# Token rows ahead of the rank matmuls, RWKV keys and solves by halves of the heads, nine loads ahead of a branch

## The chip, the cores and the metric

The kernel runs on one core of one Trainium2 chip. The metric is device time in microseconds from launch to end, the median of several runs. A profiled execution, taken beside them, shows what each engine did: TensorE (PE, with its weight loads PEld), VectorE (DVE), ScalarE (ACT), GpSimd (POOL) and SyncE (SP, which issues most DMA transfers).

## The reference

A block of two layers over 256 latent tokens and 256 context tokens of width 1024, all in float32. Layer 0 mixes the tokens by attention, layer 1 by RWKV-7, and each is followed by a mixture of 16 experts of which a token uses two. Cut to what the change touches:

```python
# after each mixer, on all tokens (512 in layer 0, the 256 latent ones in layer 1)
hl = modulate(rmsnorm(xl, norm_ffn_g[i]), ml[3], ml[4])
probs = softmax(h @ router_w)                       # 16 experts
sel   = (probs + router_bias)                       # choose a group, then two experts in it
expert_idx, gate_w = route(tokens, router_w, router_bias)
f = moe_ffn(tokens, expert_idx, gate_w, w1, w3, w2) # (silu(x @ w1) * (x @ w3)) @ w2 per expert

# RWKV: 16 heads of 64, two directions, state S of 64 x 64 per head
r, k, v = mix(0) @ w_r, mix(2) @ w_k, mix(3) @ w_v
kk = k * k_k, normalised per head
for each direction d, token t:
    sa = S @ (-kk_t)
    S  = S * decay_t + outer(sa, kk_t * iclr_t) + outer(v_t, k_d_t)
    y_t = S @ r_t
```

The kernel does not run that recurrence token by token. It cuts the 512 tokens of each direction into chunks of 64; within a chunk the products of the decayed `kk` with `kk * iclr` form a triangular 64 x 64 matrix per head, which is inverted, and a scan over the chunks uses the inverses.

## The kernel before, in words

The program is written as a sequence of stages, and a scheduler that simulates the engines orders each engine's queue from it; the order in which the stages are written decides most of it, and rotating buffers the rest.

*Routing and token rows (`route`, `moe`).* `route` (line 606) takes the router's logits, transposes them (L611), and on VectorE runs a chain of some forty small operations to the chosen experts as one-hot rows `ob` (L662). The rank matmuls (L669), 14 in layer 0 and 5 in layer 1, count how many tokens ahead of each chose the same expert. `moe` then makes the *token rows*: for each tile `t` of 128 tokens (four in layer 0, two in layer 1) and each half `n` of the width, a diagonal matrix `dg` of the norm's factors times the rows (L854, in layer 1 L857), in layer 0 plus a one-row product that adds the shift (L855), copied by ScalarE to `mhh`, and its rounding remainder by a subtraction on PE (L859) to `mhl`. The gather (L1877, L1878 in layer 0; L1049, L1050 in layer 1) picks the rows of each expert with one-hot matmuls, and so needs all token rows.

*Experts of layer 0 (`experts0`).* 16 experts in an order that the data decides, the first eight with room for 128 tokens, the others 64. Weights come in loads of 1 MB (L132, on SP's queue) into a ring of nine buffers, are split into a high and a low part (ScalarE L139, VectorE L140) for the first eight, and go to PE (L145 to L147, L1896). After the twelfth of them (`a == 11`) stands `overflow` (line 932): a conditional block (L939) for tokens over an expert's room, which is not entered with this data, but every engine evaluates its flag, and SP's queue is drained there.

*RWKV.* The string list at line 1177 is the order of the stages: `l` the low-rank projections, `K`, `R`, `V` projections, `H0` to `H3` the decayed tensors ("hats") and their products for the four tiles `u` of 128 tokens (`wkv_hat`), `S0` to `S3` the triangular solves, one for a tile with all 16 heads (`wkv_solve`), `c0` to `c7` the scan over chunks, `M` and `n` the output. The products (L1566) use 64 of the 128 columns of PE; the two chunk halves `lc` of a tile go one after the other to the same columns and into a PSUM tile each. A solve copies the products to VectorE's layout with a transpose (L1593), does 31 steps of a multiplication (L1600) and an addition (L1602), transposes twice (L1604, L1605), and ends with two rounds of small matmuls (L1624, L1628). The hats' products L1653 of the scan alternate between the two halves of the columns.

*Order around the changes.* SP issues loads in program order and stops at the first one whose buffer is not free. All engines run their queues in order.

Of the kernel before, what the change touches and what calls it, by code (L numbers as in the profile page):

```python
# [79 lines left out]
class Net:  # L80
# [525 lines left out]
    def route(self, wk, layer, T):  # L606
# [18 lines left out]
        V.tensor_tensor(out=lg, in0=p2[:, :32 * T].rearrange("p (t e) -> p t e", t=T)[:, :, 0:16], in1=bc(rs), op=ALU.mult)  # L625
        lv = lg.rearrange("p (v t) e -> p v t e", t=2)
# [200 lines left out]
    def moe(self, layer, sf):  # L827
        nc, I, F = self.nc, self.I, self.ffn
        T, cap, t0 = (4, 128, 0) if layer == 0 else (2, 64, 2)
        with ExitStack() as sm:  # L830
# [4 lines left out]
            with ExitStack() as s:  # L835
# [6 lines left out]
                r = self.route(F["rp"], layer, T)  # L842
# [4 lines left out]
                for t in range(T):  # L847
                    dg = wk.tile([128, 128], F32, tag="dg", bufs=2, name=self.uid("dg"))
                    nc.scalar.activation(dg, self.ident, AF.Copy, scale=rs[:, t:t + 1])
                    for n in range(2):  # L850
# [8 lines left out]
                        nc.tensor.matmul(p, neg, hh[:, t, ns], start=False, stop=True, skip_group_check=True)  # L859
                        nc.scalar.activation(hl[:, t, ns], p, AF.Copy)  # L860
            sf.close()
# [267 lines left out]
    def rwkv(self, st, se, sf):  # L1129
# [41 lines left out]
        self.AB, V, y = [], [], []  # L1171
# [5 lines left out]
        for o in ["l", "K", "h", "H0", "R", "H1", "Vm", "gate", "V", "hx", "close", "S0", "S1", "c0", "H2", "c1", "H3", "x", "S2", "S3", "c2", "c3", "M4", "n", "c4", "M5", "c5", "M6", "c6", "M7", "c7", "F"]:  # L1177
# [23 lines left out]
            elif o == "K":  # L1201
                self.proj_k(h)
# [10 lines left out]
            elif o[0] == "H":  # L1213
                q = int("0011"[u])
                self.AB.append(vp[q].tile([128, 2, 16, 64], F32, tag="AB", bufs=2 if q == 0 else 2, name=self.uid("AB")))
                self.wkv_hat(u, self.AB[-1])
            elif o[0] == "S":
                self.wkv_solve(vp[int("0101"[u])], u, self.AB[u])
# [111 lines left out]
    def proj_k(self, h):  # L1330
        mh, ml = self.mix_split(2, h)
        for n in range(4):
# [163 lines left out]
    def wkv_hat(self, u, AB):  # L1496
# [3 lines left out]
        for d in range(2):  # L1500
# [9 lines left out]
            for kh in range(2):  # L1510
                wk = self.hp[(2 * d + kh) % len(self.hp)]
                ks = slice(4 * kh, 4 * kh + 4)
                kk = self.ht(wk, "kk", [128, 2, 4, 128])
                nc.sync.dma_start(out=kk, in_=self.kks[:, :, ks, seg, ts])
                if lat:
                    rr = self.ht(wk, "rr", [128, 4, 128])
# [494 lines left out]
```

## Time and profile before

| | us |
|---|---|
| median of three runs | 2009.86 (2005.5 to 2012.11) |
| profiled execution | 2008.92 |
| its span, first to last instruction | 2007.1 |
| mean granted clock of TensorE | 0.93 |

The stages in the profile's time, from the span's start: conditioning and attention 0 to 325; first routing and token rows 325 to 372; experts of layer 0 372 to 935; RWKV 935 to 1505 with its projections to 1198 and solves and scan to 1452; second routing, rows and branch 1505 to 1532; experts of layer 1 to the end.

A row of a stretch gives the busy time of each engine in it. The granted clock is the share of full speed that TensorE was given: 1.00 is 2.4 GHz, 0.50 is 1.2 GHz, what lies between is a mean over both. The DMA share is the mean busy share of the 16 DMA engines. In a row in time, the text in brackets is the idle time of the engine just before, and who ended it.

### The profile page before, as it was taken

What the parts mean: (1) busy time and instruction counts of PE and PEld (TensorE: products, weight loads), DVE (VectorE), ACT (ScalarE), POOL (GpSimd) and SP (SyncE); (2) the same over time, 40 slices, a digit from 0 to 9 for tenths busy, and PEclk for the clock granted to TensorE, in tenths of its full rate; (3) what the DMA queues carried; (4) which work ended last, traced back from release to release, by engine and by line L of the source; (5) the groups of instructions that cost most, each with busy time, mean ns of one, the idle gap of its engine ahead of it and who ended that gap; (6) DMA issues with size and microseconds to landing.
All of it is one profiled execution on the core that took longest, in us unless ns stands there. A gap on an engine that the chain in (4) does not pass through costs nothing. (4 is left out here: it accounts for less than half of the span.)

```text
span 2007.1 us, 30401 instructions
## 1 busy us (share of the span) xinstructions
PE 1741.1 (87%) x11729; PEld 1060.6 (53%) x11729; DVE 957.7 (48%) x1801; ACT 738.0 (37%) x1432; POOL 318.9 (16%) x306
## 2 busy tenths in 40 slices
PE   5979998999999998995699897889967999988986
PEld 3845574665556556552277777778753333322321
DVE  2466654465555555456843688985453111110101
ACT  2234542454454544442554777643132010000000
POOL 1040031000000000005455635330230000000000
PEclk7989997799999998998698998889978999999999
DMA  8376863289999996994455779754295999999996
GB/s 328 105 295 254 268 177 112 93 337 409 406 410 355 395 410 252 385 410 185 115 189 188 249 220 273 215 142 97 86 396 201 409 409 409 409 409 409 409 409 268
DMA packets 229570, 577.04 MB, mean 287 GB/s; under 512 B 42859, under 2 KB 87171, under 8 KB 229413
## 3 DMA queue, kind: packets, MB, share of 16 engines
q1 hardware_dynamic: 212726, 543.48, 73.4%
q10 hardware_dynamic: 15536, 27.28, 3.8%
q0 software_dynamic: 1152, 4.19, 0.6%
q8 instruction: 97, 1.59, 0.3%
q14 instruction: 59, 0.48, 0.1%
HBM read 537.38 MB, written 37.54 MB: 286 GB/s over the span
## 5 line engine op out<-in xcount | busy, mean ns | idle before, releaser
L140 DVE TENSOR_TENSOR lo<-raw,hi 128x512 fp32r<-128x512 f32 x456 | 301.2, 710 | 207.5 <-ACT hi L139 201.5
L139 ACT ACTIVATE hi<-raw 128x512 fp32r<-128x512 f32 x488 | 289.2, 627 | 167.2 <-PE ps L147 116.4
L1063 PE MATMUL ps<-raw,XT 128*64 128x512 f32 x1024 | 234.3, 597 | 16.7 <-DMA raw<-in_moe_w_dram 16.7
L1063 PEld LDWEIGHTS ps<-raw,XT 128*64 128x64 f32 x1024 | 72.0, 136 | 172.5 <-issue 123.1
L1069 DVE TENSOR_TENSOR h<-h,ps 128x512 f32<-128x512 f32 x16 | 11.0, 687 | 306.2 <-PE ps L1063 306.2
L1081 PE MATMUL ps<-raw,hT 128*64 128x512 f32 x512 | 118.7, 600 | 16.0 <-DVE hT L1074 9.4
L1896 PE MATMUL ps<-raw,XT 128*64 128x512 f32 x512 | 120.7, 602 | 0.2 <-DMA raw<-in_moe_w_dram 0.2
L145 PE MATMUL ps<-hi,xh 128*128 128x512 f32 x256 | 101.1, 415 | 18.8 <-ACT hi L139 11.5
L146 PE MATMUL ps<-lo,xh 128*128 128x512 f32 x256 | 105.6, 412 | 1.7 <-DVE lo L140 1.6
L147 PE MATMUL ps<-hi,xl 128*128 128x512 f32 x256 | 102.7, 401 | 0.0
L886 POOL DMA_INDIRECT yk<-ybuf,cidx x8 | 7.8, 972 | 596.0 <-issue 596.0
L256 POOL TENSOR_TENSOR rs<-rs,mh 128x2 f32<-128x2 f32 (+2 forms) x5 | 4.3, 851 | 528.2 <-DVE rs L255 528.1
L1081 PEld LDWEIGHTS ps<-raw,hT 128*64 128x64 f32 x512 | 34.7, 136 | 79.6 <-issue 52.8
L145 PEld LDWEIGHTS ps<-hi,xh 128*128 128x128 f32 x256 | 49.3, 195 | 44.2 <-ACT hi L139 20.6
L224 PE MATMUL ps<-raw,cv 128*32 128x256 f32 x768 | 62.2, 425 | 9.4 <-DMA raw<-in_ada_w_dram 5.9
L1896 PEld LDWEIGHTS ps<-raw,XT 128*64 128x64 f32 x512 | 32.4, 136 | 60.1 <-issue 57.1
L146 PEld LDWEIGHTS ps<-lo,xh 128*128 128x128 f32 x256 | 49.8, 194 | 25.6 <-DVE lo L140 8.2
L1068 ACT ACTIVATE h<-ps 128x512 f32<-128x512 f32 x16 | 9.6, 597 | 143.1 <-PE ps L1063 143.1
L1085 ACT ACTIVATE ye<-ps 128x512 f32<-128x512 f32 x16 | 9.6, 597 | 140.1 <-PE ps L1081 140.1
L1896 PE MATMUL ps<-raw,hT 128*64 128x512 f32 x256 | 58.7, 599 | 0.8 <-DVE hT L1952 0.8
L145 PE MATMUL ps<-hi,th 128*128 128x512 f32 x128 | 48.4, 406 | 8.6 <-ACT hi L139 8.5
L147 PEld LDWEIGHTS ps<-hi,xl 128*128 128x128 f32 x256 | 49.9, 195 | 9.6
(471 smaller groups left out, 3570.4 us busy)
## 6 DMA issues: line engine op xcount, KB each, us to landing
raw<-in_moe_w_dram SPq DMA_DIRECT2D x384, 1024.0 KB
raw<-in_ada_w_dram SPq DMA_DIRECT2D x48, 1024.0 KB
kk<-kks SPq DMA_DIRECT2D x16, 512.0 KB
hB<-BK SPq DMA_DIRECT2D x16, 512.0 KB
BKm<-hB SPq DMA_DIRECT2D x16, 512.0 KB
raw<-in_attn_w_in_dram SPq DMA_DIRECT2D x6, 1024.0 KB
raw<-in_attn_w_out_dram SPq DMA_DIRECT2D x8, 512.0 KB
ybuf<-ye ACTq DMA_DIRECT2D x8, 512.0 KB
```

The lines of the kernel that those rows point to most:

```text
L139: nc.scalar.activation(hi, src, AF.Copy)
L140: (lo_eng or nc.vector).tensor_tensor(out=lo, in0=src, in1=hi.bitcast(F32), op=ALU.subtract)
L145: mm(out, lh, rh, start=start, stop=False, skip_group_check=True)
L146: mm(out, lh, rl, start=False, stop=False, skip_group_check=True)
L147: mm(out, ll, rh, start=False, stop=stop, skip_group_check=True)
L224: nc.tensor.matmul(p[32 * q:32 * q + 32, :], self.cv[:, k, :], w[:, a, q * 256:(q + 1) * 256], start=(k == 0), stop=(k == KT - 1), skip_gr ...
L1063: nc.tensor.matmul(acc[64 * n:64 * n + 64, :], XT[:, k, e % 4 * 64:e % 4 * 64 + 64], w[:, a, n * 512:(n + 1) * 512], start=(k == 0), stop= ...
L1068: nc.scalar.activation(h, hs[0], AF.Silu)
L1069: nc.vector.tensor_tensor(out=h, in0=h, in1=hs[1], op=ALU.mult)
L1081: nc.tensor.matmul(acc[64 * n:64 * n + 64, :], hT[:, k % 4, (k // 4) * 64:(k // 4) * 64 + 64], w[:, a, n * 512:(n + 1) * 512], start=(k == ...
L1085: nc.scalar.activation(ye, acc, AF.Copy)
L1896: nc.tensor.matmul(acc[0][64 * n:64 * n + 64, :], lhs(k), w[:, a, ns], start=(k == 0), stop=(k == KT - 1), skip_group_check=True)
```

## The change

Three edits. First, `route` takes a function `rows(t)` that makes the token rows of tile `t`; it issues the first half of the tiles ahead of the rank matmuls, and the second half behind them, held in that order by `issue_after`. Second, in RWKV the projection of the keys, the hats and the solves are cut by halves of the heads (`kh`): a solve now covers eight heads of two tiles (`S00`, `S01` for tiles 0 and 1, `S10`, `S11` for 2 and 3) instead of sixteen of one, so that each has the same size; the products of both chunk halves `lc` go into one PSUM tile, to partitions 0 to 63 and 64 to 127, in alternation. Third, nine loads are issued ahead of the overflow branch.

```diff
     def route(self, wk, layer, T, rows):
 ...
+        last = [rows(t) for t in range(T // 2)][-1]
         lv = lg.rearrange("p (v t) e -> p v t e", t=2)
 ...
-        for t in range(T + 1):
-            for u in range(min(t + 1, T)):
-                nc.tensor.matmul(pk[:, t, :], bf[:, 0 if u == t else 1, :], ob[:, u, :], start=(u == 0),
-                                 stop=(u == min(t, T - 1)))
+        with self.tc.issue_after(last.ins):
+            for t in range(T + 1):
+                for u in range(min(t + 1, T)):
+                    rank = nc.tensor.matmul(pk[:, t, :], bf[:, 0 if u == t else 1, :], ob[:, u, :], start=(u == 0),
+                                            stop=(u == min(t, T - 1)))
+        with self.tc.issue_after(rank.ins):
+            for t in range(T // 2, T):
+                rows(t)
 ...
-                r = self.route(F["rp"], layer, T)
 ...
-                for t in range(T):
+
+                def rows(t):
                     dg = wk.tile([128, 128], F32, tag="dg", bufs=2, name=self.uid("dg"))
 ...
+                    return mm
+                r = self.route(F["rp"], layer, T, rows)
 ...
-        for o in ["l", "K", "h", "H0", "R", "H1", "Vm", "gate", "V", "hx", "close", "S0", "S1", "c0", "H2", "c1", "H3", "x", "S2", "S3", "c2", "c3", ...
+        for o in ["l", "K0", "h", "H00", "H10", "K1", "H01", "R", "H11", "Vm", "gate", "V", "hx", "close", "S00", "S01", "c0", "H20", "H30", "c1", "H21", "H31", "x", "S10", "S11", "c2", "c3", ...
 ...
-                self.wkv_solve(vp[int("0101"[u])], u, self.AB[u])
+                q, kh = int(o[1]), int(o[2])
+                self.wkv_solve(vp[kh], self.AB[q, kh])
 ...
-    def proj_k(self, h):
-        mh, ml = self.mix_split(2, h)
-        for n in range(4):
+    def proj_k(self, mh, ml, ns):
+        for n in ns:
 ...
+            p = self.ps((128, 4, 128), tag="G")
+            for q in range(4):
                 for lc in range(2):
-                    p = self.ps((128, 4, 128), tag="G")
-                    q64 = slice(64 * d, 64 * d + 64)
-                    for q in range(4):
-                        nc.tensor.matmul(p[q64, q, :], BK[:, lc, q, Bs] if d == 0 else A[:, lc, q, :],
-                                         Abd[:, lc, q].rearrange("p a t -> p (a t)"),
-                                         start=True, stop=True, skip_group_check=True)
-                    pq = p.rearrange("p q (a t) -> p (q a) t", a=2)
-                    for jb in range(2):
-                        rows = slice(64 * d + 32 * jb, 64 * d + 32 * jb + 32)
-                        nc.scalar.activation(AB[rows, lc, 8 * kh:8 * kh + 8, 0:64 - 32 * jb],
-                                             pq[rows, :, 32 * jb:64], AF.Copy)
+                    nc.tensor.matmul(p[64 * lc:64 * lc + 64, q, :], BK[:, lc, q, Bs] if d == 0 else A[:, lc, q, :],
+                                     Abd[:, lc, q].rearrange("p a t -> p (a t)"),
+                                     start=True, stop=True, skip_group_check=True)
+            pq = p.rearrange("p q (a t) -> p (q a) t", a=2)
+            for lc in range(2):
+                for jb in range(2):
+                    to, fr = 64 * d + 32 * jb, 64 * lc + 32 * jb
+                    nc.scalar.activation(AB[to:to + 32, lc, :, 0:64 - 32 * jb], pq[fr:fr + 32, :, 32 * jb:64], AF.Copy)
 ...
-        TI = self.AB[u][:, lc]
+        TI = [self.AB[u // 2, kh][:, u % 2, lc] for kh in range(2)]
 ...
                 if a == 11:
+                    for _ in range(9):
+                        k, t = next(self.wgen)
+                        self.have[k] = t
                     self.overflow(None, 0, r, hh, hl, gate, 4, 128, 0, wk)
```

In the rest of `wkv_hat` the loop over `kh` has become an argument, and the lines stand one level further out.

PE's queue in the first routing before (`ob` the chosen experts, `dg` the diagonal of the norm's factors, `one` the row of ones, `mhh` the rows, `oh` the gather's one-hot rows; the 14 rank matmuls are L669):

```order
L611 MATMUL ps_2844<-C,lt 128x128
L669 MATMUL ps_2907<-ob,bf 128x16
...
L854 MATMUL ps_2968<-hrow,dg_2966 128x512
L855 MATMUL ps_2968<-Brow,one_2964 128x512
...
L859 MATMUL ps_3016<-mhh,neg 128x512
```

The same place now, where the rank matmuls are L671, the pairs L859 and L860, and the subtraction L864:

```order
L611 MATMUL ps_2848<-C,lt 128x128
L859 MATMUL ps_2857<-hrow,dg_2855 128x512
L860 MATMUL ps_2857<-Brow,one_2846 128x512
...
L864 MATMUL ps_2877<-mhh,neg 128x512
...
L671 MATMUL ps_2939<-ob,bf 128x16
...
L859 MATMUL ps_2956<-hrow,dg_2954 128x512
L860 MATMUL ps_2956<-Brow,one_2846 128x512
...
L864 MATMUL ps_2976<-mhh,neg 128x512
```

Four pairs and four subtractions moved ahead of the ranks, four of each stay behind; the subtractions now stand in blocks of four instead of between the pairs.

VectorE's queue at the end of the first solve before (`W` and `T` the solve's two operations, `vo` the copy of a value projection, the last pair of which stands here; `S` the next solve's first transpose):

```order
L1397 COPY vo_10669<-ps_10527 128x512
L1602 TENSOR_TENSOR T_10710<-T_10710,W_10711 128x9x23
L1397 COPY vo_10675<-ps_10529 128x512
L1600 TENSOR_TENSOR W_10711<-S_10709,T_10710 128x192
...
L1593 STREAM_TRANSPOSE S_10928<-AB_10077 128x1024
L1602 TENSOR_TENSOR T_10710<-T_10710,W_10711 128x31
L1604 STREAM_TRANSPOSE TV_10779<-T_10710 128x32x32
```

The same place now (solve L1608, L1610, its last transposes L1612, L1613; copies of the value projections L1407; hats L1545 to L1568; splits of weights L140):

```order
L1608 TENSOR_TENSOR W_10703<-S_10701,T_10702 128x31
L1545 TENSOR_TENSOR A_9806<-kk_9786,Ep_9792 128x4x2x64
L1610 TENSOR_TENSOR T_10702<-T_10702,W_10703 128x31
L1612 STREAM_TRANSPOSE TV_10771<-T_10702 128x32x32
L1613 STREAM_TRANSPOSE TU_10770<-T_10702 128x32x32
...
L1407 COPY vo_10509<-ps_10367 128x512
L1407 COPY vo_10515<-ps_10369 128x512
...
L1407 COPY vo_10667<-ps_10521 128x512
L1601 STREAM_TRANSPOSE S_10920<-AB_9737 128x1024
```

The first solve now ends ahead of all four copies of the value projections; the second begins right behind them.

VectorE's queue ahead of the overflow branch now (`fi` is the flag; `xl` the gather's remainder). Before, the load of the flag stood behind the last of the `xl` rows, and all splits L140 of the following loads behind the branch:

```order
L140 TENSOR_TENSOR lo_7498<-raw_6454,hi_7497 128x512
L1938 TENSOR_TENSOR h_6170<-h_6170,ps_6298 128x512
L140 TENSOR_TENSOR lo_7505<-raw_6456,hi_7504 128x512
L1888 TENSOR_TENSOR xl_6346<-ps_6396,xh_6345 128x256
...
L945 TENSOR_LOAD fi
L946 COMPARE_AND_BRANCH
```

The four splits of the first of the nine loads and one of the second now stand ahead of it, in the middle of the gather.

## Rows read from the trace of the kernel before

**Rows 1.** The page's busy times: us (share of the span) x instructions.

```profile
PE 1741.1 (87%) x11729; PEld 1060.6 (53%) x11729; DVE 957.7 (48%) x1801; ACT 738.0 (37%) x1432; POOL 318.9 (16%) x306
```

**Rows 2.** Stretches: busy us of PE, PEld, DVE, ACT, POOL (instructions), granted clock, DMA share, GB/s.

```profile
325.00:372.00 47.00, 37.27 (x65) 11.46 (x61) 13.47 (x74) 11.30 (x23) 0.42 (x1) 0.55 0.19 74
1140.00:1170.00 30.00, 30.00 (x171) 24.90 (x170) 14.33 (x22) 23.00 (x51) 9.97 (x13) 1.00 0.86 274
1198.00:1367.00 169.00, 139.38 (x2618) 126.42 (x2616) 152.51 (x306) 101.98 (x196) 68.14 (x85) 0.86 0.76 204
1367.00:1452.00 85.00, 81.38 (x1639) 70.52 (x1640) 37.42 (x56) 24.24 (x41) 13.95 (x11) 1.00 0.29 75
```

**Rows 3.** PE in time, first routing: start, us, line, operation [idle before it].

```profile
326.14 0.33 PE L611 MATMUL ps<-C,lt 128*128 128x128 f32 x1 [0.39 <-DVE lt L790]
334.39 0.52 PE L669 MATMUL ps<-ob,bf 128*128 128x16 bf16 x14 [7.93 <-DVE ob L662]
334.76 2.05 PE L854 MATMUL ps<-hrow,dg 128*128 128x512 f32 x2
336.75 2.07 PE L855 MATMUL ps<-Brow,one 1*128 1x512 f32 x2
...
368.08 2.50 PE L859 MATMUL ps<-mhh,neg 128*128 128x512 f32 x5
372.13 0.66 PE L1877 MATMUL ps<-oh,mhh 128*128 128x384 f32 x1 [1.55 <-issue]
```

**Rows 4.** Stretches as in rows 2, chosen for the clock.

```profile
340.00:350.00 10.00, 10.00 (x11) 2.50 (x10) 0.00 (x0) 2.00 (x4) 0.00 (x0) 0.50 0.00 0
1047.00:1051.00 4.00, 4.00 (x12) 2.48 (x11) 0.03 (x1) 0.69 (x1) 0.00 (x0) 0.63 0.55 205
1518.00:1520.00 2.00, 2.00 (x7) 0.86 (x5) 0.00 (x0) 1.35 (x3) 0.00 (x0) 1.00 0.02 4
```

**Rows 5.** PE in time, four-row matmuls of the keys, before the clock fell.

```profile
1044.33 1.98 PE L1366 MATMUL ps<-rT,C 4*128 4x512 f32 x4
```

**Rows 6.** PE in time, second routing.

```profile
1513.40 0.28 PE L669 MATMUL ps<-ob,bf 128*128 128x16 bf16 x5 [7.02 <-DVE ob L662]
1513.54 5.67 PE L857 MATMUL ps<-Xl,dg 128*128 128x512 f32 x8
1518.64 1.75 PE L859 MATMUL ps<-mhh,neg 128*128 128x512 f32 x4
1526.09 0.55 PE L1049 MATMUL ps<-oh,mhh 128*128 128x256 f32 x1 [5.70 <-DVE oh L1125]
```

**Rows 7.** Stretches as in rows 2, around the overflow branch.

```profile
755.00:765.00 10.00, 10.00 (x47) 7.25 (x46) 5.19 (x9) 4.67 (x8) 0.00 (x0) 1.00 0.00 0
838.00:912.00 74.00, 70.00 (x299) 43.03 (x297) 42.88 (x69) 39.65 (x69) 0.00 (x0) 0.98 1.02 409
```

**Rows 8.** Waits of SP from 748 to 800: total us, times, longest.

```profile
SPq L939 <- SPq L939: 21.7, 3, 14.4
SPq L132 <- DVE lo L140: 16.8, 2, 14.0
```

**Rows 9.** Lines of DVE from 1198 to 1367: busy us, mean ns | idle before.

```profile
L1600 DVE TENSOR_TENSOR W<-S,T 128x60 f32<-128x60 f32 (+15 forms) x104 | 42.4, 412 | 2.2
L1602 DVE TENSOR_TENSOR T<-T,W 128x60 f32<-128x60 f32 (+15 forms) x104 | 40.2, 390 | 2.3
```

**Rows 10.** PE in time, one pass each of two products of the same shape.

```profile
1161.34 1.96 PE L1566 MATMUL ps<-Abd,A 128*64 128x128 f32 x16
...
1379.38 1.97 PE L1653 MATMUL ps<-hatA,BKm 128*64 128x128 f32 x32
```

**Rows 11.** DVE in time, last solve's last transpose and two scan steps.

```profile
1360.95 0.68 DVE L1729 COPY X<-ps 128x512 f32<-128x512 f32 x1
1364.79 1.93 DVE L1605 STREAM_TRANSPOSE TU<-T 128x1024 f32<-128x1024 f32 x1
...
1384.08 0.69 DVE L1729 COPY X<-ps 128x512 f32<-128x512 f32 x1 [1.97 <-PE ps L1724]
```

More of the change, by code (lines that the diff above doesn't have):

```diff
@@ L604, in first_max, with route @@
         nc.vector.tensor_tensor(out=oh, in0=pr, in1=m.unsqueeze(2).to_broadcast([128, T, n]), op=ALU.is_equal)
-    def route(self, wk, layer, T):
+    def route(self, wk, layer, T, rows):
         nc, I, F = self.nc, self.I, self.ffn
@@ new lines, in wkv_hat @@
+            icl = self.ht(wk, "icl", [128, 4, 128])
+            nc.sync.dma_start(out=icl, in_=self.ics[seg][:, d, ks, ts])
+            Ep = self.ht(wk, "Ep", [128, 4, 2, 65])
+            Em = self.ht(wk, "Em", [128, 4, 2, 65])
+            for k0 in (0, 2):
+                p = self.ps((128, 2, 130), tag=self.trit)
+                for q in range(2):
+                    nc.tensor.matmul(p[:, q, :], sig[:, (k0 + q) * 128:(k0 + q + 1) * 128], tri,
+                                     start=True, stop=True)
+                pv = p.rearrange("p k (c t) -> p k c t", c=2)
+                nc.scalar.activation(Ep[:, k0:k0 + 2], pv, AF.Exp, scale=-CD)
+                nc.scalar.activation(Em[:, k0:k0 + 2], pv, AF.Exp, scale=CD)
@@ new lines, in wkv_hat @@
+            nc.gpsimd.tensor_copy(fm[:, 0, :, ks].rearrange("p c k -> p k c"), Ep[:, :, :, end])
+            nc.gpsimd.tensor_copy(fm[:, 1, :, ks].rearrange("p c k -> p k c"), Em[:, :, :, mid])
+            hA = self.hA[d, u]
+            A = self.ht(wk, "A", [128, 2, 4, 64])
+            nc.vector.tensor_tensor(out=A.rearrange("p c k t -> p k c t"), in0=v4(kk[:, 0]),
+                                    in1=Ep[:, :, :, ex], op=ALU.mult)
+            nc.sync.dma_start(out=hA[:, :, 0, ks, :], in_=A)
@@ new lines, in wkv_hat @@
+            kb = kk[:, 0]
+            diag = A if d == 0 else BK[:, :, :, Bs]
+            nc.vector.scalar_tensor_tensor(out=kb, in0=icl, scalar=-1.0, in1=kb, op0=ALU.mult, op1=ALU.mult)
+            nc.vector.tensor_tensor(out=bk(Bs), in0=v4(kb), in1=Em[:, :, :, inc], op=ALU.mult)
+            for par in range(2):
+                rows = slice(64 * par, 64 * par + 64)
+                nc.scalar.activation(Abd[rows, :, :, par, :], diag[rows], AF.Copy)
+            for q in range(4):
+                k = 4 * kh + q
+                nc.scalar.activation(icl[:, q, :], icl[:, q, :], AF.Identity, scale=self.vc[:, 56 + k:57 + k],
+                                     bias=self.omka[:, k:k + 1])
@@ new lines, in wkv_hat @@
+            pq = p.rearrange("p q (a t) -> p (q a) t", a=2)
[3 more added lines that the diff above has]
+                    nc.scalar.activation(AB[to:to + 32, lc, :, 0:64 - 32 * jb], pq[fr:fr + 32, :, 32 * jb:64], AF.Copy)
+            if lat:
+                nc.gpsimd.tensor_tensor(out=rr, in0=kd, in1=rr, op=ALU.mult)
+                pbn = self.ps((128, 8), tag="G")
+                for k in range(4):
+                    nc.tensor.matmul(pbn[:, 2 * k:2 * k + 2], rr[:, k, :], self.rk2[:, 4 * kh + k, :],
+                                     start=True, stop=True, skip_group_check=True)
+                bon = self.bon[:, tt - 2, 8 * kh:8 * kh + 8]
+                if u == 2:
+                    nc.vector.tensor_copy(bon, pbn)
+                else:
+                    nc.vector.tensor_tensor(out=bon, in0=bon, in1=pbn, op=ALU.add)
```

112 lines of the change are left out of this document (37 added, 75 removed).

## The prediction

> **What bounds the kernel now.** I read the page's busy times first. TensorE works 87% of the span [rows 1], which would suggest that only fewer matmuls could help; but that is a mean over stages with different limits, so the second view was the stretches. Four places matter.
>
> In the first routing PE waits for VectorE's chain up to `ob` for 7.93 us, then makes the token rows from 334.76 to 368.08 + 2.50 = 370.58, which is 35.8 us of unbroken work, and the gather of the experts follows at 372.13 [rows 3]. All of it runs at a granted clock of 0.50, the lower of the two levels (1.2 GHz), although PE is busy in 10.00 of 10.00 us [rows 4]. In 325 to 372 the DMA share is 0.19 [rows 2]: the ring of weights is full, and nothing but PE moves.
>
> Around the overflow branch the weight stream stands still, share 0.00 for ten microseconds, while PE still has loaded weights; later, from 838, the stream is the limit with a share of 1.02 [rows 7]. SP's own waits at the branch are 21.7 us [rows 8].
>
> In the RWKV layer PE is full in 1140 to 1170 while VectorE has 15.7 of 30 us free; from 1198 to 1367 it is the other way, VectorE 152.5 of 169 us and PE 139.4 at clock 0.86; from 1367 to 1452 PE is full again, 81.4 of 85 us [rows 2].
>
> In the second routing PE waits 7.02 us, makes the rows in 5.67 and 1.75 us, and waits 5.70 us for the branch [rows 6]. The expert stages behind both routings are chains that begin with the gather, so a gather that starts earlier moves all behind it.
>
> **First routing.** The matmuls are the same: eight pairs of a 128-row and a one-row product, 4.0 us a pair at half clock (334.76 to 338.75; the two records are 2.05 and 2.07), and eight subtractions, together the 35.8 us [rows 3]. Four pairs and four subtractions, half of it, now stand ahead of the rank matmuls. Their inputs are there when the transpose at 326.14 ends, so they can begin at 326.5 and lie beside VectorE's chain. The added wait, rank behind the first half, holds up VectorE's short chain on the ranks; that is done 5 us after the ranks, well inside the second half's 9 to 18 us, so it costs nothing.
> What the clock does decides the price. At half clock throughout, the first half ends at 326.5 + 17.9 = 344.4, the ranks (0.5) and the second half at 362.8: 7.8 us earlier, which is just the idle time that is filled. At full clock throughout, halves of 9 us end at 335.5 and 345.0: 25.6 earlier, and the gather, whose first pass now still shows 0.66 us, would begin at full clock too, for which I allow 2.5 (an estimate): 28. In between, full clock at the start (the mean of 0.55 over 325 to 372 leaves room for a little of it [rows 2]) and a fall during or at the end of the first half: 335.5 + 0.5 + 17.9 = 353.9, 16.7 earlier. I take the case between, 17, for two reasons. PE no longer stands idle for 7.93 us ahead of the rows; and there is a row in which the clock falls while PE is full: behind four passes of a product with only four rows (1.98 us) it is 0.63 in 1047 to 1051 with PE busy in 4.00 of 4.00 us [rows 4, 5]. Half of the token rows' time is in products with one row. Range 8 to 28.
>
> The Trainium skill says otherwise ("TensorE: Matmul & The Clock Gate", section "Part 1: The HAM clock gate"): the throttled state is the default and activity releases it, so an engine that is never idle should keep the full clock. By that rule this term would be 28. The trace agrees in the second routing, where the clock is 1.00 by 1518 with only 128-row products ahead, and disagrees in the first, 0.50 at 10.00 of 10.00 us busy [rows 4]; the rule is therefore a rival below, not the forecast.
>
> **Nine loads ahead of the branch.** They fill the hole in the stream: a load of 1 MB takes 2.56 us at 409 GB/s [rows 7], nine take 23 us, so counted from 755 the ring is full by about 778. But then SP must wait for free buffers, as it does now for 14.0 us behind VectorE's splits [rows 8], because these still come behind the branch. The hole is moved more than removed. What stays is what VectorE now splits ahead of the branch, one load and a little: one or two loads of 2.56 us, 4 us. Bounds: 8 if the hole (10 us at least) is mostly gone; -4 if the five splits of 0.7 us push the branch later on VectorE. The rest of the stage is limited by the stream, so the gain holds.
>
> **RWKV.** Two things become earlier. First, the decayed products: one pass of 16 matmuls takes 1.96 us in L1566, and L1653, of the same shape but alternating between the two halves of the columns, makes 32 in 1.97 us [rows 10]. The products now alternate so too: 1.0 us less a pass. The first eight of the sixteen passes lie in the stretch that PE bounds, so 8 us; the rest lies under VectorE's work. Second, the solve of the first eight heads needs only the first half of the keys and stands wholly ahead of the last value projections; before, 104 pairs of solve operations came after 1198, of which 93 are the three later solves (31 each), so 11 pairs of the first, (412 + 390) ns each, and its two transposes of 1.93 us [rows 9, 11], 13 us, leave the stretch that VectorE bounds for one where it has 15.7 us free in 30 [rows 2]. Together 21 us. The counts of all else stay: hats, solves and scan have the instructions that they had, only in another order, and ScalarE copies the products in four pieces a pass as before, now between partition ranges, with 102 of 169 us busy [rows 2]. I cost these at nothing; were ScalarE slower at it by half, VectorE's queue would still hide it.
> Against it stands a new wait. A solve now holds half the heads of two token tiles, so the fifth scan step (c4) needs both late solves; before it needed only the third. Before, c4 had its X at 1360.95 + 0.68 = 1361.6, the last solve's transpose ended at 1366.7 and its matmuls at 1379.38, between scan work [rows 10, 11]. Alone I estimate these at 8 of the 12.7 us. The last solve then ends at 1374.7 - 21 = 1354, and c4 goes on 1361.6 - 1354 = 8 us earlier, so 13 of the 21 us are given back. Since the solve's matmuls no longer lie inside c4 to c7, 2 us more: 10. Upper end 25: c4 does not wait, and the solve's 4 us leave the last stretch. Lower end: VectorE gains nothing, the last solve ends at 1379.4 - 8 = 1371, 10 us late, and the second half of the keys, whose normalising chain now stands between the products with fewer projections to cover it, costs PE 5 us: -15.
>
> **Second routing.** Two of four row products and their subtractions fit into the 7.02 us of idle time; the whole now takes 6.9 us, from 1513.54 to 1518.64 + 1.75. The other half would take 3.4 of the same mix of clocks; I take 4.4, since it begins after a wait: 2.5 (0 if the branch rather than the rows sets the 1526.09, 4 if the clock is full from its start) [rows 6].
>
> **Sum.** 17 + 4 + 10 + 2.5 = 33.5 us. The profiled execution took 2008.9 us, so 1975.4; the median of the runs is 0.9 above it: 1976.
>
> **Rivals.**
> Full clock through the rows. For it: PE is busy from the first row to the gather, and the second routing's clock rose under such work. Against it: 36 us at half clock [rows 3, 4]. Time: 11 us less, 1965; with RWKV near its upper end about 1955. It is the skill's rule of above at work.
> The solves give nothing. For it: VectorE's queue is in order, and the early solve stands among the splits that the projections wait for; c4's new wait. Against it: VectorE's free time in 1140 to 1170 [rows 2]. RWKV at -7 (solves at their old place, last end 10 us late, 3 back from the products), the rest as forecast: 1976 + 17 = 1993.
> Slower than before: the last solve holds the scan. If the hats and splits that now stand between the halves push its last transpose back instead of forward, c4 to c7, 81.4 us of full PE at clock 1.00 [rows 2], start late. The other three terms give 23.5, so it decides from a solve end 23.5 us behind 1361.6, at 1385, which is 6 us later than now. At 10 us later c4 is 27 us late, and if the clock falls in that wait, 20 us of scan work at half clock cost 20 more: 47 lost, 2033. Against it: nothing was added to VectorE's work, and its free time lies ahead of the solves.
> The change does little: rows at half clock at once and the hole only moved (8 + 0), RWKV at -7: within 2 us of now, 2009.
>
> **How the numbers follow.** Forecast 0.53 (own range 1964 to 1987), full clock 0.21, solves give nothing 0.14, no change 0.06, slower 0.06. The range takes in the first three but for their far ends (below 1954 about 0.04, above 2000 about 0.14, the last two cases and a little of the third): 1954 to 2000. A difference under 0.3%, 6 us, cannot be told from none in this kernel. Faster: 0.53 + 0.21 + 0.14 = 0.88; the remaining 0.12 is 0.06 and 0.06.
>
> **What would show it.** The first routing: token rows start at 326.5 and their clock falls within the first half; the last subtraction ends near 354 (345 if the rival is right, 363 if the clock is low throughout). The branch: SP's share of 0.00 is gone from behind the branch, and a new hole of some 10 us stands 20 us later. RWKV: passes of 16 products take about 1.0 us; the first solve's last transpose stands ahead of the last value projection; c4's second product waits for the last solve's copies. The forecast is wrong if the gather starts less than 8 us earlier, or if the time from the end of the last value projection to the end of the scan (1198 to 1452) grows.

## The result: 0.9% slower

The changed kernel takes 2025.06 us in the median of 17 runs (2012.33 to 2032.37), the kernel before 2006.07 (1997.14 to 2012.81): a ratio of 1.0086, with a 95% interval of 1.0066 to 1.0106. The forecast was 1976 us. The profiled execution has a span of 2024.7 us at a mean granted clock of 0.917, against 2007.1 at 0.930.

The first routing gained what was forecast and a little more. PE in time in the changed kernel (the pairs are L859 and L860 now, the ranks L671, the subtractions L864, the gather L1885):

```profile
325.62 0.33 PE L611 MATMUL ps<-C,lt 128*128 128x128 f32 x1 [0.39 <-DVE lt L795]
325.79 1.02 PE L859 MATMUL ps<-hrow,dg 128*128 128x512 f32 x2
...
334.11 1.89 PE L864 MATMUL ps<-mhh,neg 128*128 128x512 f32 x4
335.81 0.58 PE L671 MATMUL ps<-ob,bf 128*128 128x16 bf16 x14
...
340.14 1.12 PE L860 MATMUL ps<-Brow,one 1*128 1x512 f32 x2
341.19 2.08 PE L859 MATMUL ps<-hrow,dg 128*128 128x512 f32 x2
...
349.20 2.08 PE L864 MATMUL ps<-mhh,neg 128*128 128x512 f32 x4
352.82 0.66 PE L1885 MATMUL ps<-oh,mhh 128*128 128x384 f32 x1 [1.55 <-issue]
```

The 7.93 us of idle time of [rows 3] are gone. The four pairs of the first half run at full clock (1.02 us for what took 2.05). The clock falls at 334.4, under the four subtractions that end this half; it is back at 1.00 from 337.8 to 341.2, and then at 0.50 until 358.3. The gather starts at 352.82 instead of 372.13. The stretches of the changed kernel show the same clock, and the branch: the ten microseconds with a share of 0.00 in [rows 7] are gone, but the stream is thin later, down to 0.33:

```profile
330.00:334.00 4.00, 4.00 (x8) 1.08 (x8) 3.55 (x20) 1.59 (x3) 0.00 (x0) 1.00 0.93 382
342.00:346.00 4.00, 4.00 (x5) 1.00 (x4) 0.00 (x0) 0.60 (x1) 0.00 (x0) 0.50 0.00 0
755.00:765.00 10.00, 7.28 (x39) 5.32 (x37) 4.03 (x8) 3.91 (x14) 0.00 (x0) 0.97 0.58 214
780.00:785.00 5.00, 5.00 (x24) 2.67 (x23) 3.27 (x5) 3.03 (x5) 0.00 (x0) 1.00 0.33 90
1105.00:1132.00 27.00, 16.18 (x77) 11.95 (x78) 14.38 (x32) 13.34 (x25) 12.22 (x9) 0.51 0.54 180
1193.00:1456.00 263.00, 210.08 (x4033) 192.32 (x4034) 169.56 (x317) 116.62 (x222) 78.84 (x95) 0.80 0.58 151
```

The last two rows are where the time went. In 1105 to 1132 PE works 16.18 of 27 us at a clock of 0.51, in the middle of the projections. PE in time there, and ahead of it the start of RWKV's projections (L1161, the transpose of the layer's vectors):

```profile
927.21 0.41 PE L1161 MATMUL ps<-C,vr 88*128 88x88 f32 x1 [17.96 <-DVE yk L938]
...
1110.61 3.58 PE L1362 MATMUL ps<-C,ksq 128*128 128x2 f32 x16 [4.42 <-ACT Em L1540]
1117.21 1.97 PE L1574 MATMUL ps<-Abd,A 128*64 128x128 f32 x16 [3.02 <-ACT Abd L1563]
...
1120.90 3.78 PE L1376 MATMUL ps<-rT,C 4*128 4x512 f32 x4 [0.77 <-DVE rT L1373]
1124.61 3.58 PE L1362 MATMUL ps<-C,ksq 128*128 128x2 f32 x16
1130.79 0.48 PE L1497 MATMUL ps<-C,gs 128*128 128x128 f32 x1 [2.60 <-ACT gs L1495]
1131.55 0.78 PE L145 MATMUL ps<-hi,mxh 128*128 128x512 f32 x1
```

L1362 and L1376 are the normalising chain of the second half of the keys, L1574 the products of the hats; the value projection (L145, last row) stands behind all of it in PE's queue, at 1131.55. The same marks in the kernel before, with the X of its first two scan steps:

```profile
952.08 0.41 PE L1154 MATMUL ps<-C,vr 88*128 88x88 f32 x1 [17.39 <-DVE yk L931]
1202.40 0.68 DVE L1397 COPY vo<-ps 128x512 f32<-128x512 f32 x1
1240.40 0.68 DVE L1729 COPY X<-ps 128x512 f32<-128x512 f32 x1
1262.97 0.68 DVE L1729 COPY X<-ps 128x512 f32<-128x512 f32 x1
```

RWKV's projections began 24.9 us earlier than before (927.21 and 952.08), but the last copy of a value projection is only 10.4 us earlier, at 1191.96 instead of 1202.40.

From there to the eighth scan step's X the changed kernel needs 263 us (row above), the kernel before 232. VectorE in time, `X` and `UV` being the marks of a scan step, L1601 and L1612 the start and the end of a solve:

```profile
1191.96 0.69 DVE L1407 COPY vo<-ps 128x512 f32<-128x512 f32 x1 [0.67 <-PE ps L147]
1201.10 1.94 DVE L1601 STREAM_TRANSPOSE S<-AB 128x1024 f32<-128x1024 f32 x1 [8.45 <-DMA vs<-vo]
1220.87 0.68 DVE L1737 COPY X<-ps 128x512 f32<-128x512 f32 x1
1224.29 0.69 DVE L1770 COPY UV<-ps 64x512 f32<-64x512 f32 x1
1265.02 2.05 DVE L1612 STREAM_TRANSPOSE TV<-T 128x1024 f32<-128x1024 f32 x1
1298.12 0.69 DVE L1770 COPY UV<-ps 64x512 f32<-64x512 f32 x1
1311.77 0.72 DVE L1737 COPY X<-ps 128x512 f32<-128x512 f32 x1
```

The first scan step has its X at 1220.87 and finishes heads 0 to 7 at 1224.29. Heads 8 to 15 come 74 us later, at 1298.12: they need the second solve, which begins at 1201.10 and whose steps stand between those of the later hats until 1265. The next X is 91 us behind the first. In the kernel before it was 23 (1240.40 and 1262.97).

At the second routing the ranks now end 3.94 us of idle time instead of 7.02 in [rows 6], and the gather is 18.5 us behind the transpose instead of 20.0.

By stages, the two traces differ so: from the first transpose (L611) to the gather 18.8 us less, from there to the start of RWKV 5.5 less, to the last value projection 14.4 more, to the eighth X 31.3 more, and from there to the second gather 2.6 less.

### The profile page after: what moved, and what is told of

Same layout as the page of the kernel before. It is cut to its first block, busy times and chain, and to the rows that moved or that the text cites. A ratio compares the mean times of both kernels' runs of the same rounds, so it can differ in the third digit from the quotient of the medians.

```text
span 2024.7 us, 30406 instructions
## 1 busy us (share of the span) xinstructions
PE 1740.9 (86%) x11729; PEld 1062.5 (52%) x11729; DVE 967.6 (48%) x1801; ACT 741.7 (37%) x1434; POOL 316.5 (16%) x306
## 5 line engine op out<-in xcount | busy, mean ns | idle before, releaser
L140 DVE TENSOR_TENSOR lo<-raw,hi 128x512 fp32r<-128x512 f32 x456 | 304.9, 714 | 217.7 <-ACT hi L139 216.4
L145 PE MATMUL ps<-hi,xh 128*128 128x512 f32 x256 | 101.6, 417 | 12.7 <-ACT hi L139 8.9
L145 PEld LDWEIGHTS ps<-hi,xh 128*128 128x128 f32 x256 | 49.1, 194 | 41.0 <-ACT hi L139 18.5
L1610 DVE TENSOR_TENSOR T<-T,W 128x31 f32<-128x31 f32 (+15 forms) x124 | 54.8, 442 | 3.3 <-DVE W L1608 0.2
L145 PE MATMUL ps<-hi,th 128*128 128x512 f32 x128 | 48.6, 406 | 7.5 <-ACT hi L139 7.3
```

The costliest lines, as they stand in the source:

```text
L140: (lo_eng or nc.vector).tensor_tensor(out=lo, in0=src, in1=hi.bitcast(F32), op=ALU.subtract)
L145: mm(out, lh, rh, start=start, stop=False, skip_group_check=True)
L1610: nc.vector.tensor_tensor(out=T[:, j + 1:32, 0:m], in0=T[:, j + 1:32, 0:m], in1=w, op=ALU.add)
```

## The experiments

Ratios are to the kernel before, in runs on the same chip.

**The parts alone.** The first and third edit on the kernel before, and the RWKV edit on the kernel before (the diff of the change above, split).

> The kernel before with the first and third edit alone (token rows ahead of the rank matmuls, nine loads ahead of the branch); RWKV as before. The trace of the changed kernel has the first gather 19 us earlier, the branch stage 3 to 6 us more ahead, the second routing 1.5 us. If these gains are real and the whole loss is in the RWKV edit: 23 to 28 us faster than before, near 1981. If gains at the front are given back by later stages that wait for something else: under 10 us.

> The kernel before with the RWKV edit alone. If the RWKV edit alone costs what the two traces show between the start of the RWKV projections and the second routing: 40 to 48 us slower than before, near 2050. If the loss comes from how the RWKV stage meets the earlier stages (weights that are already loaded, another phase of the clock): under 25 us slower.

Measured: 1973.13 us, ratio 0.9813 (0.978 to 0.9846), for the first and third edit; 2053.82 us, ratio 1.0251 (1.0208 to 1.0294), for the RWKV edit. The first is more than I expected, and it beats both kernels; the second is the loss of some 50 us. In the first the stretch from the last value projection to the eighth X, and the same in the kernel before:

```profile
1175.00:1403.00 228.00, 201.72 (x4046) 184.76 (x4045) 171.26 (x336) 120.91 (x226) 82.38 (x95) 0.90 0.66 176
```

```profile
1203.00:1435.00 232.00, 201.16 (x4033) 184.29 (x4032) 175.35 (x336) 120.84 (x226) 80.91 (x95) 0.90 0.65 173
```

So without the RWKV edit the last value projection is 28 us earlier, and the changed kernel's loss of some 52 us against this one is 18 in the projections (1193 instead of 1175) and 35 in the scan (263 instead of 228).

**The wait of the first scan step.** In the changed kernel, the first steps take the first solve's tile for all heads:

```diff
-        TI = [self.AB[u // 2, kh][:, u % 2, lc] for kh in range(2)]
+        TI = [self.AB[u // 2, kh if u >= 2 else 0][:, u % 2, lc] for kh in range(2)]
```

> The changed kernel, but the first four scan steps take the inverses of heads 8 to 15 from the first solve's tile instead of the second's, so that they do not wait for the second solve; all work is still done, the results of these steps are not the reference's. If the wait for the second solve is what costs (the first scan step's second half stood from 1224 to 1292): 20 to 35 us faster than the changed kernel, so 5 to 15 us faster than before. If the loss is in the projections (15 us) and the rest in VectorE's load: under 10 us faster than the changed kernel, still slower than before.

Measured: 1997.51 us, ratio 0.9953 (0.9933 to 0.9972): 28 us less than the changed kernel. VectorE in time: the first step's second UV, the next X.

```profile
1220.83 0.68 DVE L1737 COPY X<-ps 128x512 f32<-128x512 f32 x1
1224.24 0.69 DVE L1770 COPY UV<-ps 64x512 f32<-64x512 f32 x1
1225.74 0.69 DVE L1770 COPY UV<-ps 64x512 f32<-64x512 f32 x1
1246.49 0.68 DVE L1737 COPY X<-ps 128x512 f32<-128x512 f32 x1
```

The work is the same and the wait is gone. The last value projection is not earlier (1193.91 + 0.69), so the gain lies in the scan. It is not the price of the wait alone: the scheduler has ordered VectorE's queue anew as well, and about a quarter of its rows in RWKV stand elsewhere.

**The halves of the keys.** The two halves of the key projection next to each other again, all else as in the changed kernel:

```diff
-"l", "K0", "h", "H00", "H10", "K1", "H01", "R", "H11", ...
+"l", "K0", "K1", "h", "H00", "H10", "H01", "R", "H11", ...
```

> The changed kernel with the two halves of the key projection next to each other again, ahead of all hats; solves by halves of the heads as in the changed kernel. If the normalising chain of the second half of the keys, between hats and without projections beside it, costs the 18 us: the last copy of a value projection moves from 1192 to 1165 to 1178, but the first scan step still waits for the second solve: 8 to 20 us faster than the changed kernel, 2005 to 2017. If the early first solve on VectorE delays the projections instead: little change of that copy, within 6 us of the changed kernel.

Measured: 1992.01 us, ratio 0.9933 (0.9911 to 0.9955): 33 us less than the changed kernel, more than forecast. The last copy of a value projection is at 1171.40, 20 us earlier, as the first theory said; the scan is shorter too, 246 us:

```profile
1172.00:1418.00 246.00, 209.21 (x4049) 189.39 (x4050) 181.84 (x342) 121.91 (x228) 80.86 (x96) 0.83 0.61 163
```

Its first step still waits for the second solve, with 49 us between the copies of its two halves of the heads and 79 us between the first two X:

```profile
1201.98 0.69 DVE L1737 COPY X<-ps 128x512 f32<-128x512 f32 x1
1216.39 0.69 DVE L1770 COPY UV<-ps 64x512 f32<-64x512 f32 x1
1265.11 0.69 DVE L1770 COPY UV<-ps 64x512 f32<-64x512 f32 x1
1281.32 0.72 DVE L1737 COPY X<-ps 128x512 f32<-128x512 f32 x1
```

So the wait can stand in a kernel that is faster than the one before. The remaining 13 us are not told apart further.

**Halved keys with whole solves.** Hats by halves of the heads as in the changed kernel, but into a tile of all 16 heads, and a solve for each tile:

```diff
-                q, kh = int(o[1]), int(o[2])
-                self.wkv_solve(vp[kh], self.AB[q, kh])
+                self.wkv_solve(vp[u % 2], self.AB[u])
```

> The changed kernel with the solves by tile as before (16 heads of one tile), but keys and hats by halves of the heads. If the wait for the second solve costs 27 us and the halved keys 18 us before the last value projection: the 18 us stay (last copy of a value projection near 1192), the 27 come back, though the first solve now needs the late half of the keys: 10 to 30 us faster than the changed kernel, 1995 to 2015. If halved solves are needed for halved keys to pay (the first solve early): no faster than the changed kernel.

Measured: 2009.29 us, ratio 1.0019 (1.0001 to 1.0037): 16 us less than the changed kernel, with the last copy of a value projection at 1193. The loss in the projections stays without the halved solves, so it belongs to the halved keys. The scan has 246 us here.

**The second solve's pool.**

```diff
-                self.wkv_solve(vp[kh], self.AB[q, kh])
+                self.wkv_solve(vp[0 if q == 0 else kh], self.AB[q, kh])
```

> The changed kernel, with the second solve's work tiles in the pool of the first, which exists from the start, instead of the one that is made from the projections' memory after their last transfer. The second solve's first transpose stood 8.5 us idle behind that transfer. If that start is what makes the second solve late: its end 6 to 10 us earlier and the kernel 5 to 10 us faster. If it is the work of the later hats between its steps on VectorE: its end within 4 us, the kernel the same as the changed one, 2020 to 2028.

Measured: 2023.44 us, ratio 1.008 (1.0049 to 1.0112), as the changed kernel. The second solve started no earlier (1207.84), because it now waited for the matmuls of the first solve in the same tiles (6.71 us idle, ended by L1636). That its end moved by only 4 us therefore tells nothing of the 8.45 us.

**The paired products alone.** In the kernel before, `wkv_hat`'s inner loop as in the change:

```diff
-                for lc in range(2):
-                    p = self.ps((128, 4, 128), tag="G")
-                    q64 = slice(64 * d, 64 * d + 64)
-                    for q in range(4):
+                p = self.ps((128, 4, 128), tag="G")
+                for q in range(4):
+                    for lc in range(2):
...
```

> The kernel before with only the decayed products changed: both chunk halves into one PSUM tile, alternating between the two halves of the columns; keys, hats and solves as before. My step said 1.0 us less for each of sixteen passes, 8 of them on the path: 5 to 10 us faster, a pass about 1.0 us in the profile. A rival says that the copies between partition ranges or the order cost as much: no difference, or up to 10 us slower.

> The kernel before with the first and third edit and the paired products, with neither halved keys nor halved solves. If the gains add up: 37 and 6 us, near 1965, 2 to 2.3% faster than before. If the paired products gain nothing once the stages ahead stand elsewhere: as the first and third edit alone, 1973.

> The first and third edit, with the paired products only for the first two tiles, which are made beside the projections, and the single products for the later two, which are made beside the solves. If pairing pays where PE is the limit and disturbs the scan only where the later tiles are made: the projections' 8 us remain and the scan is as with single products, near 1965. If what was lost with all products paired (15 us against the first and third edit alone) comes from the order that the scheduler then gives to solves and scan from the start: 1980 to 1990.

Measured alone: 2001.71 us, ratio 0.997 (0.9943 to 0.9997): 6 us, with 1 to 11 in the interval, as forecast. A pass takes 1.09 us in the changed kernel:

```profile
1174.80 1.09 PE L1574 MATMUL ps<-Abd,A 128*64 128x128 f32 x16
```

With the first and third edit: 1988.0 us, ratio 0.9904 (0.9883 to 0.9925), and with pairing for the first two tiles only 1994.31, ratio 0.9949 (0.9923 to 0.9974). Both are slower than the first and third edit without pairing. The gains do not add up, and it is not the later tiles. The last value projection is 8 us earlier (1167 instead of 1175), the amount worked out, but only 2.8 of it arise between the start of RWKV and there (245.1 us instead of 247.9); the scan is 250 us long instead of 228:

```profile
1167.00:1417.00 250.00, 210.11 (x4050) 192.45 (x4050) 182.11 (x345) 124.30 (x233) 82.02 (x96) 0.83 0.62 159
```

**The RWKV edit in its parts.** The runs so far can be put side by side. All four of the table have the first and third edit and the paired products; without the pairing it is 1973.13 us, with a scan of 228.

| us (scan) | solves by tile | solves by halves of the heads |
|---|---|---|
| keys whole | 1988.0 (250) | 1992.01 (246) |
| keys by halves | 2009.29 (246) | 2025.06 (263) |

From 1973 to the changed kernel it is 52 us. Pairing costs 15 of them, all in the scan. Halved keys cost 21, or 33 beside halved solves; halved solves cost 16, or 4 beside whole keys, which the intervals do not tell from none. By the ratios it is 18, 23 (31) and 13 (6). The scan is some 20 us longer than 228 with solves by tile too, so the wait of the first step cannot be the price of the whole 35 us.

**The edits at the front, one by one.**

> The kernel before with the first edit alone. By the stages of the trace: the gather of layer 0 19 to 21 us earlier, the second routing 1.5 us: 20 to 23 us faster, about 1985. If the 37 us of the first and third edit together belong to the rows (a later stage that falls into a better phase): 28 us or more.

> The kernel before with the nine loads ahead of the branch alone. By the stages of the trace: 4 to 6 us faster, about 2000. If the loads are what makes the two edits together worth 37 us: 10 us or more. If the hole in the stream is only moved: no difference.

Measured: 2010.76 us, ratio 1.0018 (0.9997 to 1.0039), for the token rows alone, and 2005.48, ratio 0.9998 (0.9981 to 1.0016), for the loads alone. Neither gains anything by itself, and together they gain 37 us. The traces show how. In the token rows alone PE in time at the second half of the rows, a stretch there, and the scan:

```profile
344.64 1.25 PE L864 MATMUL ps<-mhh,neg 128*128 128x512 f32 x4
347.43 0.66 PE L1884 MATMUL ps<-oh,mhh 128*128 128x384 f32 x1 [1.54 <-DVE cwm L885]
```

```profile
339.00:345.00 6.00, 6.00 (x14) 1.79 (x13) 2.29 (x16) 1.47 (x4) 0.00 (x0) 1.00 0.00 0
1174.00:1433.00 259.00, 212.67 (x4042) 192.96 (x4041) 175.67 (x337) 120.69 (x226) 79.30 (x95) 0.86 0.60 155
```

The last value projection is as early as with both edits, 1174. But that is partly luck: in this execution the clock stayed at 1.00 through all token rows, the one-row products among them, and the gather came 21.2 us behind the transpose (326.28), against 27.2 in the changed kernel and 46.0 before. The loads do gain in their stage: from the gather to the start of RWKV the ten traces with nine loads take 570.3 to 574.8 us (median 574.3), the six without 574.8 to 579.9 (median 578.0). In the loads alone a scan of 239 us instead of 232 takes that back. And in the token rows alone the scan takes 259 us instead of 228, with the same code. The order in which the scheduler has put solves, hats and scan steps into the queues is another one: the end of the second solve stands ahead of the second scan step's X on VectorE; in the kernel before, and with both edits, it stands behind. So I held that pair by hand, first with the token rows alone, then with all but the halves:

```diff
-            nc.vector.tensor_tensor(out=w, ...
+            with self.tc.issue_after(behind.ins) if behind is not None and j == 24 else ExitStack():
+                nc.vector.tensor_tensor(out=w, ...
...
-"S0", "S1", "c0", "H2", "c1", "H3", ...
+"S0", "c0", "H2", "c1", "S1", "H3", ...
```

> The first edit alone, with one order held: the last seven steps and the closing transposes of the second solve stand behind the second scan step on VectorE, as in the kernel before; with the first edit alone the scheduler had put them ahead of it, and the scan from the last value projection took 259 us instead of 232. If that order is what took back the 29 us won at the front: 15 to 28 us faster than before, 1980 to 1992. If the longer scan has another cause (loads, clock): no difference to before, as without the order held.

> The first and third edit and the paired products, with the same order held. Without it: 1988, with the scan at 250 us from the last value projection. If the order of the second solve and the second scan step decides: 10 to 25 us faster than that, 1963 to 1978. If the paired products lengthen the scan in themselves: 1985 to 1990.

Measured: 2007.7 us, ratio 1.0017 (0.9994 to 1.004), and 1994.54, ratio 0.9943 (0.992 to 0.9967). My theory of this one pair falls: the second X did come 23 us behind the first, but the wait moved to the fourth, 57 us behind the third, and the scan was 256 us long.

What was left was the order as a whole, or the loads after all. With eight and with six loads instead of nine the queues of RWKV come out known: with eight, VectorE's is row by row that of nine; with six it is nine tenths that of the kernel before.

```diff
-                    for _ in range(9):
+                    for _ in range(8):      # and 6
```

> The first edit with eight loads ahead of the branch instead of nine. VectorE's queue in RWKV is then, row by row, that of the first edit with nine loads. If the order of the queues sets the length of the scan: 228 us from the last value projection to the last scan step as there, 1970 to 1978. If the loads themselves carry the gain: one load less, 2.6 us, 1975 to 1980. This one alone does not tell the two apart, the next does.

> The first edit with six loads ahead of the branch. VectorE's queue in RWKV is then nine tenths that of the kernel before, and three quarters that of the first edit with nine loads. If the order of the queues sets the length of the scan: 228 to 238 us as before (232), so that most of the 29 us at the front comes through, 1975 to 1985. If the loads carry the gain, from 2011 with none to 1973 with nine: two thirds of the way, 1984 to 1990, with the scan at about 238 to 242 us.

Measured: 1980.64 us, ratio 0.9867 (0.9832 to 0.9902), and 1976.37, ratio 0.9837 (0.9804 to 0.987). The scan with eight, and with six:

```profile
1177.00:1402.00 225.00, 200.39 (x4047) 182.27 (x4046) 170.89 (x336) 120.62 (x226) 82.63 (x95) 0.91 0.67 178
```

```profile
1179.00:1402.00 223.00, 195.89 (x4036) 180.69 (x4034) 173.60 (x336) 121.73 (x226) 80.77 (x95) 0.92 0.69 180
```

Six loads gain as much as nine, and queues in the order of the fast kernels give the fast scan. Nor do the loads set the scan's length themselves: the kernel before has none and a scan of 232 us, and with nine loads and the paired products it is 250. So the number of loads seems to matter only in that it moves the scheduler's simulation to another order. That the order is the cause is argued from these pairs of runs; the one pair of instructions that was held by hand did not bring the short scan back, and which feature of the order is the good one stays open.

**The clock in the token rows.** In the kernel before, each one-row product replaced by one of 128 rows:

```diff
-                            nc.tensor.matmul(p, one, F["B"][:, t // 2, ns], ...
+                            nc.tensor.matmul(p, dg, F["h"][:, t, ns], ...
```

> The kernel before, where in the first routing's token rows each one-row product is replaced by a second product of 128 rows with the same columns (the rows then lack the shift and hold the norm twice). If the one-row products hold the clock at half: it rises to 1.00 within the rows and these take 18 to 26 us instead of 35.8. If the clock stays low for another reason (what came before, the instruction's type): the rows take 34 to 37 us at 0.50.

Measured: one run, 1993.4 us. PE in time, and the stretch from 340:

```profile
334.15 2.06 PE L854 MATMUL ps<-hrow,dg 128*128 128x512 f32 x2
...
337.64 1.02 PE L854 MATMUL ps<-hrow,dg 128*128 128x512 f32 x2
...
350.19 1.75 PE L859 MATMUL ps<-mhh,neg 128*128 128x512 f32 x4
```

```profile
340.00:345.00 5.00, 5.00 (x14) 2.30 (x13) 0.00 (x0) 2.91 (x7) 0.00 (x0) 1.00 0.00 0
```

The same number of products, at the same place, rises to full clock after 3.5 us and is done in 17.8 us instead of 35.8 [rows 3]. With products of 128 rows in the place of the one-row ones the clock does not stay at half. With the one-row products, the four traces whose rows start behind the wait (the kernel before, the loads, the products and the RWKV edit alone) stay at 0.50 for 28 us of the rows at least.

## Why the prediction was wrong, point by point

*First routing: right in size, its reason only in part.* Forecast 17 us, 16.7 for a fall at the end of the first half; measured 19.3 at the gather. The clock stayed at 1.00 through the pairs of the first half and was back there for 3.4 us of the second, so it lies between the two bounds, near the one that I took. The reason was that one-row products pull the clock down. Behind the wait they go with half clock, and without them the same rows rise to 1.00; but issued ahead of it, the same rows in the same order ran at 1.00 to the end in the trace of the token rows alone. There the gather is 24.8 us nearer to the transpose than before, which is the full-clock rival's 25.6. The other twelve traces of these rows, the changed kernel's among them, do show a fall; what decides it stays open. The Trainium skill ("TensorE: Matmul & The Clock Gate", section "Part 1: The HAM clock gate") would have had it at full clock throughout; the trace of the token rows alone agrees, at 1.00 with PE busy in 6.00 of 6.00 us (339 to 345), and that of the changed kernel does not, at 0.50 in 4.00 of 4.00 us (342 to 346).

*Nine loads: right in their stage.* Forecast 4 us; the stage from the gather to RWKV is some 4 us shorter with nine loads (574.3 instead of 578.0, medians of the traces), and the hole is mostly moved, as I had written. The loads alone bring no gain in the whole (ratio 0.9998), because in their trace the scan is longer.

*Second routing: right in kind, 1.5 us instead of 2.5.*

*RWKV: the step that failed.* Forecast 10 us gained; the two traces show 46 lost from the start of RWKV to the eighth X, and the runs 52 against the first and third edit alone. Three terms were wrong.
First: "costs PE 5 us", the price of the halved keys' normalising chain, which I set as part of a lower end. It cost about 20: whole keys bring the last value projection from 1192 to 1171. I had priced the chain's matmuls and not the queue: the value projection stood behind it, so each wait in between (4.42 us ahead of the chain for ScalarE, 3.02 and 2.60 of the hats and the gate, 0.77 for VectorE) was a wait of PE, and its work there ran at half clock. From the start of RWKV to the last value projection PE is idle for 47 us instead of 37 with whole keys, and 55 us of its work instead of 32 are at half clock, half of which is lost: 10 and 11 us.
Second: "Against it stands a new wait. A solve now holds half the heads of two token tiles, so the fifth scan step (c4) needs both late solves". The same sentence is true of the first scan step and the early solves, and I did not write it down. I saw that the first solve ends earlier (it did: 1165 instead of 1217) and called that 13 us of gain; but the scan does not get past its first step with one solve any more. The second one, which needs the late half of the keys and memory of the projections, ended as late as before, and the scan, which is a chain of eight steps of 18 to 31 us once it runs, went on behind it. What this costs depends on the rest: halved solves cost 16 us with halved keys and 4 with whole ones, where the same wait stands. The 28 us of the experiment without the wait come with another order of the queue.
Third: "The counts of all else stay: hats, solves and scan have the instructions that they had, only in another order", and "I cost these at nothing". The other order was not free. The paired products gain 6 us alone, as forecast, but behind the first and third edit they cost 15: the last value projection is 8 us earlier, and the scan 22 longer. Why that order is the slow one stays open.
The rival "the last solve holds the scan" had the nearest mechanism, a solve by halves that holds a scan step and a clock that falls in the wait, at the wrong one of the two places, and 0.06 as its chance. The prediction's own sign of being wrong did come: the time from the last value projection to the end of the scan grew.

*How the scan's length adds up.* It is the idle time of PE, plus half of the time that PE works at half clock, plus its work as it would be at full clock; the trace's record of the clock, laid over PE's instructions, gives all three. Before: 31 idle, 42 us of work at half clock, 21 of them lost, and 181 of work. After: 53 idle, 82 at half clock, 41 lost, and 170 of work. So PE's work in the scan fell by 11 us, of which the eight paired passes in it account for 7 (1.09 us instead of 1.96 each), and the waits put 42 us of idle time and slow clock in its place.

*What I did not weigh.* The scan's length, with unchanged RWKV code, lies between 223 and 259 us, as far as these runs show by the order that the scheduler finds. That is as large as the whole effect that I forecast, and my range of 1954 to 2000 held nothing for it.

## What to carry to other kernels

When a unit of work is cut the other way (half the heads of two tiles instead of all heads of one), list for each consumer which units it now needs, the first consumer before the last: an earlier first unit brings little by itself if its first reader also needs the second. Where a scheduler orders the queues, an edit at the front can reorder a stage far behind it: compare the order of the stages that were not touched, and time an edit together with small variants that only shift the schedule, before its gain or loss is put down to what it does.

## What the runs showed of the hardware

A stretch in which PE shows as busy throughout can run at half clock from end to end: token rows in which products of one row alternate with products of 128 took 35.8 us, nearly all of it at 0.50, and 17.8 us, at 1.00 from 337.6 on, when all had 128 rows. Issued right behind work at full clock, the same mixture ran its first 8 us at 1.00 before the clock fell in the changed kernel, and all of its 19 us at 1.00 in the run of the token rows alone: the same instructions in the same order can end at either level.
